# Two expert layers of a fused network: spread shared by two engines, operands loaded ahead, the second layer dense over all tokens

## The chip, the cores and the metric

One program runs on one core of one Trainium2 chip. The metric is the device time of one execution in microseconds (us). The core has five engines that each work through their own queue in order: PE (TensorE, matrix products; PEld is its weight load), DVE (VectorE), ACT (ScalarE), POOL (GpSimd) and SP (SyncE, which here issues nearly all transfers). Transfers go through 16 DMA engines.

## The reference

The network is two blocks. The first has two layers over 256 context tokens and 256 latent tokens of width 1024; each layer is a token mixer and then an expert layer (`peer_ffn`). The second block (four layers of attention or recurrence, each with a gated feed-forward part) is not touched here. An expert layer computes, per token, 8 heads x 16 chosen experts out of 16384:

```python
qr = (h @ wq).reshape(bsz, t, 8, 2, 128)
scores = jnp.einsum('bthpd,hpkd->bthpk', qr, subkeys)
s1, i1 = lax.top_k(scores[..., 0, :], 16)
s2, i2 = lax.top_k(scores[..., 1, :], 16)
cand = (s1[..., :, None] + s2[..., None, :]).reshape(bsz, t, 8, 256)
cidx = (i1[..., :, None] * 128 + i2[..., None, :]).reshape(bsz, t, 8, 256)
top, pos = lax.top_k(cand, 16)
eidx = jnp.take_along_axis(cidx, pos, axis=-1)
gate = jax.nn.softmax(top, axis=-1)
act = jax.nn.gelu(jnp.einsum('ted,td->te', u[ek], hk), approximate=False)
out = jnp.einsum('te,ted->td', gk * act, v[ek])
```

The first layer's expert part handles 512 tokens (context and latent), the second layer's the 256 latent ones only.

## The kernel before, in words

Every expert layer is computed in two ways at once (`peer`, line 883). The first F tokens are **gathered**: `fetched` (line 858) reads, per token, the 128 chosen rows of u and v with one indirect transfer on POOL's queue (tile `uv`, line 873) and does two passes over 1024 columns on DVE (lines 874 and 869). The other ND = N - F tokens are **dense**: all 16384 experts are computed for them, as 128 rows j of 128 experts, and a gate matrix that is zero where an expert was not chosen removes the rest. `FETCHED` sets F: 128 of 512 tokens in the first expert layer, 64 of 256 in the second.

Work of one expert layer, in the order of the code:

- `route` (line 719): 16 chunks of queries and scores, top-16 searches on DVE (`top16`), the choice of experts per tile of 128 tokens (`choose`), the gate values (`gates`), and `spread` (line 813). Spread builds the dense gate matrix four tokens at a time: a one-hot tile `oa` of 512 columns and four scaled one-hot tiles `ob` of 128 columns, all on DVE (lines 819 and 824), four small products on PE (line 825), and two copies out on ACT (line 828), written to DRAM tile `g` every 32 tokens.
- `ahead` (line 958) runs the **first product** of one row j beside the routing: a load `wraw` of u, and the products with all ND tokens on PE. In the first expert layer u is split into a coarse part `whi` (ACT) and a rest `wlo` (DVE), and 24 products of 384 columns follow, in threes of whi, whi, wlo (line 949). In the second layer ND is 192, the sum `xw` is used, and 8 full-precision products run without a split (line 944). The result goes to DRAM tile `u`.
- After the routing a **dense loop** goes over pairs of rows j: `u_phase` (line 983) loads gates (`gt`) and first products (`ad`) four rows at a time, applies Gelu on ACT, multiplies on DVE and splits the result into `wt`; rows that were not done ahead are computed here. `v_phase` (line 1008) loads a row of v (`wraw`, line 1013), splits it and runs the **second product**. With ND a multiple of 128 it is token-stationary: `wt` holds the weights, v streams with 512 columns (line 1026, 18 products a row in the first layer). Otherwise v holds the weights and `wt` streams with 192 columns (line 1019, 24 products a row).

What orders the work: the loop over `route` keeps two sums of estimated times, `tp` for PE and `td` for DVE, and calls `ahead` while `tp` is behind `td`; `EVERY` does the same for the gathered tokens, and what is left of those goes evenly over the dense loop. A scheduler then places the instructions of each engine; buffers rotate, so a load waits until the buffer's last reader is done.

Of the kernel before, what the change touches and what calls it, by code (L numbers as in the profile page):

```python
# [41 lines left out]
CU = (.0108, .0137)  # L42
# [4 lines left out]
FETCHED = (128, 64)  # L47
# [4 lines left out]
WORKP = (dict(nbig=2048, bufs=4, ga=3, w=(4, 3, 2), mm=2, sm=6, sp=4, uv=4, H=1, acc=1),  # L52
         dict(nbig=2048, bufs=2, ga=3, w=(6, 2, 2), mm=4, sm=4, sp=6, uv=5, H=1, acc=1, xw=1))
ROUTE = dict(bufs=3, rt=1, VI=1, t=3, r=13, alt=1, oa=2, ob=4)
DENSE = dict(bufs=1, gt=2, ad=2, wt=2, o=2)
# [28 lines left out]
class Kern:  # L84
# [634 lines left out]
    def route(self, l, xh, xl, cs, G, F, fetch):  # L719
# [93 lines left out]
        def spread(t):  # L813
            for t0 in range(*own(t), GT):
                st = [self.b8().rearrange("p (j t) -> p j t", t=GT) for _ in range(2)]
                for t4 in range(t0, t0 + GT, 4):
                    pg = self.ps()
                    a = self.t(512, tag="oa").rearrange("p (t n) -> p t n", t=4)
                    nc.vector.tensor_tensor(a, self.iotaf[:, None, :].to_broadcast([P, 4, P]),
                                            i1T[:, t4:t4 + 4, None].to_broadcast([P, 4, P]), op=OP.is_equal)  # L820
                    for i in range(4):
                        t_ = slice(t4 + i, t4 + i + 1)
                        b_ = self.t(P, tag="ob")
                        nc.vector.tensor_scalar(b_, self.iotaf, i2T[:, t_], gT[:, t_], op0=OP.is_equal, op1=OP.mult)
                        nc.tensor.matmul(pg[:, i * P:(i + 1) * P], a[:, i], b_, start=True, stop=True)
# [57 lines left out]
    def peer(self, l, extra=()):  # L883
# [8 lines left out]
        xh, xl = self.big(KD, N, F32R), self.big(KD, N, F32R)  # L892
# [35 lines left out]
        self.part(routing, **ROUTE)  # L928
# [9 lines left out]
        def u_act(j, func):  # L938
            ps = self.ps("MM")[:, :ND]
            if whole:  # L940
                raw = self.w.tile([P, 1024], F32, name="wraw", bufs=self.wb[0])
                nc.sync.dma_start(raw, A["uT"][l, j])
                for k in range(KD):
                    nc.tensor.matmul(ps, raw[:, k * P:(k + 1) * P], xw[:, k], start=k == 0, stop=k == KD - 1)  # L944
            else:
                hi, lo = self.load_w(A["uT"][l, j])
            for k in range(0 if whole else KD):
                for q, (w_, x_) in enumerate(((hi, xh), (hi, xl), (lo, xh))):
                    nc.tensor.matmul(ps, w_[:, k * P:(k + 1) * P], x_[k, dc],  # L949
                                     start=(k == 0 and q == 0), stop=(k == KD - 1 and q == 2))  # L950
            a = self.t(max(ND, D // 2), tag="ga")[:, :ND]
            self.actv(a, ps, func)
            return a


        early, tp, td = 0, 0.0, HEAD[l]

        def ahead():
            nc.sync.dma_start(U[:, early], u_act(early, AF.Copy))
        done = 0  # L960
        for pe, dve in self.route(l, xh, xl, cs, G, F, fetch):
# [3 lines left out]
            while tp < td and early < P:  # L965
                ahead()
                early, tp, td = early + 1, tp + ND * CU[l], td + (0.0 if whole else 1.1)
# [6 lines left out]
        self.part(dense, **DENSE)  # L974
        left = F - done
        J = 2

        nd = ND // P if ND % P == 0 else 0
        res = [[self.ps() for _ in range(2)] for _ in range(nd)] if nd else [self.ps() for _ in range(4)]
        half = lambda c: res[c // 2][:, c % 2 * 256:c % 2 * 256 + ND]  # L980
        held = {}

        def u_phase(j0):
            if j0 % 4 == 0:
                gt = self.t(4 * ND, tag="gt")
                held["g"] = gt.rearrange("p (b j t) -> p j b t", j=4, t=GT)
                nc.sync.dma_start(gt.rearrange("p (b j) -> p b j", b=nb),
                                  G[:, :nb, j0:j0 + 4].rearrange("p b j t -> p b (j t)"))
                if j0 < early:
# [1002 lines left out]
```

## Time and profile before

| what | value |
|---|---|
| runs of the kernel | 4761.98, 4771.15, 4781.52 us (median 4771.15) |
| the profiled execution | 4776.65 us; its span from first to last instruction 4774.9 us |
| busy over the span | PE 4352.2 us (91%), DVE 3402.8 (71%), ACT 2104.5 (44%), POOL 288.9 (6%) |
| mean granted TensorE clock | 0.953 of 2.4 GHz |
| moved | 948.85 MB, mean 199 GB/s |

The span has these stages, read from the first and last instruction of the lines above: first mixer to 385 us; first expert layer, routing and first product, 385 to 1240, its dense loop 1240 to 1836; second mixer to 2086; second expert layer, routing 2086 to 2436, its dense loop 2436 to 3108; the second block from there to the end. A share of the whole span says little here; each stage has to be read on its own.

### The profile page before, as it was taken

Reading aid. Unit: us, or ns where it says so; the run is one execution under the profiler, and the core shown is the slowest. Engines: PE = TensorE matmul, PEld = TensorE weight load, DVE = VectorE, ACT = ScalarE, POOL = GpSimd, SP = SyncE. Lnnn points to the kernel's source line nnn. Section 1 sums busy time; section 2 is a strip of 40 time slices with the busy share of each in tenths; the row PEclk is TensorE's granted clock in tenths of the full one; section 3 lists DMA queues with packets and bytes.
Section 4 is the critical chain, followed back from the end, with each engine's and each line's share of the span. In section 5 each row is a group of like instructions: output and inputs, shape, how many; then the busy total and the mean of one; then the engine's idle time right before and its main releaser. Section 6 shows DMA issues by size and latency. Waiting matters only on the chain. (4 is left out here: it accounts for less than half of the span.)

```text
span 4774.9 us, 72861 instructions
## 1 busy us (share of the span) xinstructions
PE 4352.2 (91%) x27964; PEld 3992.4 (84%) x27964; DVE 3402.8 (71%) x6651; ACT 2104.5 (44%) x4022; POOL 288.9 (6%) x200
## 2 busy tenths in 40 slices
PE   6999798998988999998967799989999999999999
PEld 5887798888876787887856699978998998899799
DVE  9987998899778757978863344477567567566765
ACT  4443344344433445541323233377445454445853
POOL 0000022222011100001220000000000000000000
PEclk8999899999999999999977799999999998999999
DMA  5413388888999874547994468533553553055255
GB/s 191 133 58 104 136 291 323 295 309 329 327 305 337 281 223 130 169 160 282 377 376 146 148 204 266 193 99 103 175 152 108 175 159 100 19 172 165 90 168 172
DMA packets 313101, 948.85 MB, mean 199 GB/s; under 512 B 28832, under 2 KB 130080, under 8 KB 282928
## 3 DMA queue, kind: packets, MB, share of 16 engines
q1 hardware_dynamic: 285104, 742.86, 47.4%
q0 software_dynamic: 27648, 201.34, 11.2%
q8 instruction: 219, 3.59, 0.3%
q14 instruction: 130, 1.06, 0.1%
HBM read 872.70 MB, written 71.04 MB: 198 GB/s over the span
## 5 line engine op out<-in xcount | busy, mean ns | idle before, releaser
L208 ACT ACTIVATE whi<-wraw 128x1024 fp32r<-128x1024 f32 (+1 forms) x924 | 964.3, 1047 | 1337.0 <-PE MM L293 524.3
L293 PE MATMUL MM<-xhl,whi 128*128 128x272 f32 (+1 forms) x4736 | 934.6, 293 | 6.7 <-ACT whi L208 6.1
L275 DVE TENSOR_TENSOR wlo<-wraw,whi 128x1024 fp32r<-128x1024 f32 (+2 forms) x668 | 799.3, 1198 | 161.2 <-PE MM L293 53.1
L293 PE MATMUL MM<-b,whi 128*128 128x272 f32 (+2 forms) x3712 | 855.3, 323 | 59.8 <-ACT b L208 50.0
L293 PEld LDWEIGHTS MM<-xhl,whi 128*128 128x128 f32 x4736 | 751.2, 190 | 27.4 <-issue 10.0
L293 PEld LDWEIGHTS MM<-b,whi 128*128 128x128 f32 x3712 | 623.0, 192 | 115.8 <-ACT b L208 56.5
L293 PE MATMUL MM<-xhl,wlo 128*128 128x272 f32 (+1 forms) x2368 | 689.2, 291 | 2.8 <-DVE wlo L275 2.7
L293 PE MATMUL MM<-b,wlo 128*128 128x272 f32 (+2 forms) x1856 | 597.2, 323 | 5.3 <-DVE wlo L275 4.7
L949 PE MATMUL MM<-b,whi 128*128 128x384 f32 x2048 | 545.4, 347 | 14.2 <-ACT ga L208 13.9
L280 DVE TENSOR_TENSOR wlo<-wraw,whi 128x1024 fp32r<-128x1024 f32 x256 | 311.3, 1222 | 277.4 <-ACT whi L208 206.4
L1019 PE MATMUL SM<-wt,whi 128*128 128x192 f32 x2048 | 399.0, 300 | 103.2 <-ACT whi L208 76.1
L293 PEld LDWEIGHTS MM<-xhl,wlo 128*128 128x128 f32 x2368 | 448.7, 190 | 10.2 <-DVE wlo L275 4.6
L873 POOL DMA_INDIRECT uv<-uv,sp x192 | 287.9, 1499 | 2676.1 <-DVE acc L869 952.0
L1019 PEld LDWEIGHTS SM<-wt,whi 128*128 128x128 f32 x2048 | 352.6, 215 | 106.9 <-ACT whi L208 79.3
L949 PE MATMUL MM<-b,wlo 128*128 128x384 f32 x1024 | 356.0, 349 | 59.0 <-DVE wlo L275 59.0
L949 PEld LDWEIGHTS MM<-b,whi 128*128 128x128 f32 x2048 | 380.2, 195 | 18.6 <-ACT ga L208 17.9
L1026 PE MATMUL SM<-whi,wt 128*128 128x512 f32 x1536 | 380.7, 397 | 13.7 <-ACT wt L208 8.0
L293 PEld LDWEIGHTS MM<-b,wlo 128*128 128x128 f32 x1856 | 355.7, 192 | 31.2 <-DVE wlo L275 10.0
L944 PE MATMUL MM<-xw,wraw 128*128 128x192 f32 x2048 | 359.1, 332 | 10.5 <-ACT ga L208 9.9
L1026 PEld LDWEIGHTS SM<-whi,wt 128*128 128x128 f32 x1536 | 293.7, 192 | 82.1 <-ACT wt L208 10.7
L944 PEld LDWEIGHTS MM<-xw,wraw 128*128 128x128 f32 x2048 | 339.7, 194 | 12.5 <-ACT ga L208 11.6
L1019 PE MATMUL SM<-wt,wlo 128*128 128x192 f32 x1024 | 305.0, 298 | 15.2 <-DVE wlo L280 15.2
(488 smaller groups left out, 6096.8 us busy)
## 6 DMA issues: line engine op xcount, KB each, us to landing
wraw<-uT SPq DMA_DIRECT2D x256, 512.0 KB
wraw<-uv SPq DMA_DIRECT2D x256, 512.0 KB
wraw<-w_gate_up SPq DMA_DIRECT2D x176, 512.0 KB
g<-b SPq DMA_DIRECT2D x36, 1024.0 KB
wraw<-w_in SPq DMA_DIRECT2D x64, 512.0 KB
wraw<-fox_w_in SPq DMA_DIRECT2D x64, 512.0 KB
wraw<-w_down SPq DMA_DIRECT2D x64, 512.0 KB
wmod<-wmodT SPq DMA_DIRECT2D x56, 512.0 KB
```

The lines of the kernel that those rows point to most:

```text
L208: r = nc.scalar.activation(out, in_, func, **kw)
L275: nc.vector.tensor_sub(lo[:, :n], raw[:, :n], hi[:, :n].bitcast(F32))
L280: self.nc.vector.tensor_sub(lo, src, hi.bitcast(F32))
L293: nc.tensor.matmul(ps, w_, x_[k, slice(a, b)], start=(i == 0 and q == 0), stop=(i == kc - 1 and q == 2))
L873: nc.gpsimd.indirect_dma_start(z, None, self.A[f"uv{l}"], bass.IndirectOffsetOnAxis(ap=ids[:, js], axis=0))
L944: nc.tensor.matmul(ps, raw[:, k * P:(k + 1) * P], xw[:, k], start=k == 0, stop=k == KD - 1)
L949: nc.tensor.matmul(ps, w_[:, k * P:(k + 1) * P], x_[k, dc], start=(k == 0 and q == 0), stop=(k == KD - 1 and q == 2))
L1019: nc.tensor.matmul(half(c), w_[:, c * P:(c + 1) * P], x_[:, jj], start=j == 0 and q == 0 and c % 2 == 0, stop=j == P - 1 and q == 2, skip_ ...
L1026: nc.tensor.matmul(res[c][h], w_[:, jj, c * P:(c + 1) * P], v[:, h * 512:(h + 1) * 512], start=(j == 0 and q == 0 and i == 0), stop=(j == ...
```

## The change

- `FETCHED` becomes (128, 0): the second expert layer gathers no tokens, and all its 256 tokens are dense. Since 256 is a multiple of 128 and above 192, its first product takes the split form (24 products of 256 columns) and its second product the token-stationary one (12 products of 512 columns a row).
- All 128 rows of the first product are done before the dense loop, in both layers; the last ones after the routing has ended. Gelu is applied as the product leaves PSUM. The products with `whi` all come first, then those with `wlo`.
- Spread: both one-hot tiles are built on DVE with 512 columns, and the scaling by the gate moves to ACT (four instructions of 128 columns for four tokens). The `oa` ring has 3 buffers in the first layer and 4 in the second.
- The dense loop loads v rows 4 (first layer) or 5 (second) rows ahead into buffers of its own (`vr`), gates 8 rows at a time and one group ahead, first products 4 rows at a time and two groups ahead.
- The normalised inputs `xh`, `xl` now lie in the memory that is freed at the end of the routing part.

```diff
-CU = (.0108, .0137)
+CU = (.0108, .0113)
-FETCHED = (128, 64)
+FETCHED = (128, 0)
-ROUTE = dict(bufs=3, rt=1, VI=1, t=3, r=13, alt=1, oa=2, ob=4)
-DENSE = dict(bufs=1, gt=2, ad=2, wt=2, o=2)
+ROUTE = (dict(bufs=7, rt=1, VI=1, t=3, r=13, alt=1, oa=3, ob=2), dict(bufs=5, rt=1, VI=1, t=4, r=16, alt=2, oa=4, ob=2, xw=1))
+DENSE = (dict(bufs=0, gt=2, ad=3, wt=2, vr=5, o=2), dict(bufs=0, gt=2, ad=3, wt=2, vr=6, o=2))
+LAST = 4
...
-                    a = self.t(512, tag="oa").rearrange("p (t n) -> p t n", t=4)
-                    nc.vector.tensor_tensor(a, self.iotaf[:, None, :].to_broadcast([P, 4, P]),
-                                            i1T[:, t4:t4 + 4, None].to_broadcast([P, 4, P]), op=OP.is_equal)
+                    ohs = []
+                    for z in (i1T, i2T):
+                        o = self.t(512, tag="oa")
+                        nc.vector.tensor_tensor(o.rearrange("p (t n) -> p t n", t=4),
+                                                self.iotaf[:, None, :].to_broadcast([P, 4, P]),
+                                                z[:, t4:t4 + 4, None].to_broadcast([P, 4, P]), op=OP.is_equal)
+                        ohs.append(o)
+                    b_ = self.t(512, tag="ob")
                     for i in range(4):
-                        t_ = slice(t4 + i, t4 + i + 1)
-                        b_ = self.t(P, tag="ob")
-                        nc.vector.tensor_scalar(b_, self.iotaf, i2T[:, t_], gT[:, t_], op0=OP.is_equal, op1=OP.mult)
-                        nc.tensor.matmul(pg[:, i * P:(i + 1) * P], a[:, i], b_, start=True, stop=True)
+                        ts = slice(i * P, (i + 1) * P)
+                        self.actv(b_[:, ts], ohs[1][:, ts], AF.Copy, scale=gT[:, t4 + i:t4 + i + 1])
+                        nc.tensor.matmul(pg[:, ts], ohs[0][:, ts], b_[:, ts], start=True, stop=True)
...
+                terms = [(hi[:, k * P:(k + 1) * P], z[k, dc]) for k in range(KD) for z in (xh, xl)]
+                terms += [(lo[:, k * P:(k + 1) * P], xh[k, dc]) for k in range(KD)]
+            for i, (w_, x_) in enumerate(terms):
+                nc.tensor.matmul(ps, w_, x_, start=i == 0, stop=i == len(terms) - 1)
             a = self.t(max(ND, D // 2), tag="ga")[:, :ND]
-            self.actv(a, ps, func)
-            return a
+            self.actv(a, ps, AF.Gelu)
+            nc.sync.dma_start(U[:, j], a)
...
-            while tp < td and early < P:
+            while tp < td and early < P - LAST:
                 ahead()
...
-        late = min(P, -(-early // 4) * 4 + 4)
-        while early < late:
+        while early < P:
             ahead()
-            early += 1
+            done += fetch_for(ND * CU[l], 10.0)
...
+        J, JU, JG = 2, 4, 8
+        def load_g(n):
+            if n < P // JG:
+                gt = self.t(JG * ND, tag="gt")
+                nc.sync.dma_start(gt.rearrange("p (b j) -> p b j", b=nb),
+                                  G[:, :nb, n * JG:(n + 1) * JG].rearrange("p b j t -> p b (j t)"))
+        def load_u(n):
+            if n < P // JU:
+                ads[n] = self.t(JU * ND, tag="ad").rearrange("p (j t) -> p j t", j=JU)
+                nc.sync.dma_start(ads[n], U[:, n * JU:(n + 1) * JU])
+        def load_v(j):
+            if j < P:
+                raws[j] = self.t(D, tag="vr")
+                nc.sync.dma_start(raws[j], A[f"uv{l}"].rearrange("(p j) d -> p j d", j=P)[:, j, D:])
+        def gated(j0):
+            if j0 % JG == 0:
+                load_g(j0 // JG + 1)
+            if j0 % JU == 0:
+                load_u(j0 // JU + 2)
+            wt = self.t(J * 2 * ND, F32R, "wt").rearrange("p (j s t) -> p j s t", j=J, s=2)
+            for jj in range(J):
+                nc.vector.tensor_mul(b3(a[:, jj]), b3(a[:, jj]), gts[j0 // JG][:, j0 % JG + jj])
+            self.split(a, wt[:, :, 0], wt[:, :, 1])
+            return wt
```

Three places in the engines' queues show what this does.

VectorE in the second expert layer, at the end of the spread (`oa`, `ob` are the one-hot tiles, `acc`, `ga` the two passes of a gathered token, `wlo` the split of a loaded row, `ad` first products times gates). Before:

```order
L819 TENSOR_TENSOR oa<-iotaf,rt 128x512
L824 TENSOR_SCALAR ob<-iotaf,rt 128x128 x4
L874 SCALAR_TENSOR_TENSOR ga,sp<-uv,H 128x1024
L869 SCALAR_TENSOR_TENSOR acc<-uv,sp,acc 128x1024
L819 TENSOR_TENSOR oa<-iotaf,rt 128x512
L824 TENSOR_SCALAR ob<-iotaf,rt 128x128 x4
L280 TENSOR_TENSOR wlo<-wraw,whi 128x1024 x2
```

And now:

```order
L823 TENSOR_TENSOR oa<-iotaf,rt 128x512 x20
L277 TENSOR_TENSOR wlo<-wraw,whi 128x1024
L823 TENSOR_TENSOR oa<-iotaf,rt 128x512 x2
L277 TENSOR_TENSOR wlo<-wraw,whi 128x1024
L823 TENSOR_TENSOR oa<-iotaf,rt 128x512 x8
L277 TENSOR_TENSOR wlo<-wraw,whi 128x1024 x81
L1015 TENSOR_TENSOR ad<-ad,gt 128x256 x4
```

The gathered tokens are gone, few splits of u stand among the spread, and 81 of the 128 rows of the first product come after it, ahead of the dense loop.

SyncE at the start of the second layer's dense loop (`gt` gates, `ad` first products, `wraw` or `vr` rows of v, `u` and `g` the DRAM tiles). Before:

```order
L831 DMA g_66<-b_20186 128x2048
L959 DMA u_68<-ga 128x192 x2
L1013 DMA wraw<-uv 128x1024
L987 DMA gt<-g_66 128x6x128
L991 DMA ad<-u_68 128x768
L987 DMA gt<-g_66 128x6x128
L991 DMA ad<-u_68 128x768
L1013 DMA wraw<-uv 128x1024
```

And now:

```order
L964 DMA u_68<-ga 128x256 x7
L993 DMA gt<-g_66 128x8x256
L964 DMA u_68<-ga 128x256
L999 DMA ad<-u_68 128x1024 x2
L1004 DMA vr<-uv 128x1024 x5
L993 DMA gt<-g_66 128x8x256
L999 DMA ad<-u_68 128x1024
```

Rows of v were already loaded before the loop began; now the first gates, first products and five rows of v are issued together at its start, and none of them earlier, since their buffers lie in the memory of the routing part.

TensorE at the end of the first product in the first expert layer (`b` are the tiles of the normalised input). Before:

```order
L949 MATMUL MM<-b_2890,whi 128x384
L949 MATMUL MM<-b_2892,whi 128x384
L949 MATMUL MM<-b_2890,wlo 128x384
L1026 MATMUL SM<-whi,wt 128x512 x12
L1026 MATMUL SM<-wlo,wt 128x512 x6
```

And now:

```order
L961 MATMUL MM<-b_2899,whi 128x384
L961 MATMUL MM<-b_2901,whi 128x384
L961 MATMUL MM<-b_2898,wlo 128x384 x4
L961 MATMUL MM<-b_2899,wlo 128x384 x4
L1031 MATMUL SM<-whi,wt 128x512 x12
L1031 MATMUL SM<-wlo,wt 128x512 x6
```

The eight products that need the rest `wlo` moved from every third place to the end of the row.

## Rows read from the trace of the kernel before

**Rows 1.** Windows: stretch, length, then busy us of each engine, clock, DMA, GB/s.

```profile
385.00:1240.00 855.00, 769.26 (x4370) 730.12 (x4371) 751.38 (x1770) 332.39 (x712) 150.37 (x92) 0.96 0.73 261
1240.00:1640.00 400.00, 354.67 (x1454) 279.13 (x1453) 321.39 (x431) 162.62 (x245) 58.33 (x36) 0.96 0.91 318
1640.00:1836.00 196.00, 195.58 (x874) 162.21 (x873) 97.09 (x117) 84.62 (x93) 0.00 (x0) 1.00 0.64 204
2086.00:2436.00 350.00, 305.89 (x1964) 295.29 (x1964) 296.28 (x807) 99.58 (x306) 51.31 (x43) 0.93 0.81 301
2436.00:2500.00 64.00, 27.72 (x140) 25.98 (x139) 42.49 (x61) 15.94 (x44) 21.30 (x14) 0.63 0.99 371
2500.00:2786.00 286.00, 203.84 (x1386) 197.64 (x1385) 100.73 (x147) 84.08 (x117) 0.00 (x0) 0.77 0.48 154
2786.00:3108.00 322.00, 322.00 (x2472) 322.00 (x2472) 150.16 (x222) 115.27 (x212) 6.56 (x7) 1.00 0.71 229
```

**Rows 2.** Waits from 2500 to 2786 us: who for whom, us, times, longest.

```profile
ACT ad L208 <- DMA ad<-u: 109.5, 15, 13.2
ACT whi L208 <- PE SM L1019: 95.2, 28, 4.8
PE SM L1019 <- ACT whi L208: 74.4, 15, 6.6
```

**Rows 3.** Groups of instructions on VectorE, the same stretch.

```profile
L280 DVE TENSOR_TENSOR wlo<-wraw,whi 128x1024 fp32r<-128x1024 f32 x58 | 69.7, 1223 | 90.2 <-ACT whi L208 90.2
```

**Rows 4.** Timeline of PE, four places: start, us, instruction.

```profile
1225.32 0.33 PE L949 MATMUL MM<-b,wlo 128*128 128x384 f32 x1
1227.92 0.33 PE L949 MATMUL MM<-b,wlo 128*128 128x384 f32 x1
...
1824.86 2.88 PE L1026 MATMUL SM<-whi,wt 128*128 128x512 f32 x12
1828.94 2.88 PE L1026 MATMUL SM<-whi,wt 128*128 128x512 f32 x12
...
2100.41 0.28 PE L293 MATMUL MM<-b,wlo 128*128 128x256 f32 x1
2100.77 0.28 PE L293 MATMUL MM<-b,wlo 128*128 128x256 f32 x1
...
2907.02 0.27 PE L1019 MATMUL SM<-wt,wlo 128*128 128x192 f32 x1
2910.37 0.27 PE L1019 MATMUL SM<-wt,wlo 128*128 128x192 f32 x1
```

**Rows 5.** Groups of instructions, second expert layer's routing, 2086 to 2436 us.

```profile
L824 DVE TENSOR_SCALAR ob<-iotaf,rt 128x128 f32<-128x128 f32 x192 | 53.9, 354 | 4.2 <-PE SM L825 4.1
L874 DVE SCALAR_TENSOR_TENSOR ga<-uv,H 128x1024 bf16<-128x1024 f32 x39 | 47.5, 1218 | 33.5 <-DMA u<-ga 24.7 <-issue 6.4 <-ACT b L208 1.3
L869 DVE SCALAR_TENSOR_TENSOR acc<-uv,sp,acc 128x1024 f32<-128x1024 f32 x37 | 47.3, 1279 | 7.7 <-ACT sp L208 7.7
L819 DVE TENSOR_TENSOR oa<-iotaf,rt 128x512 f32<-128x512 f32 x48 | 32.8, 683 | 0.0
L275 DVE TENSOR_TENSOR wlo<-wraw,whi 128x1024 fp32r<-128x1024 f32 x14 | 16.9, 1208 | 5.4 <-ACT whi L208 5.4
L208 ACT ACTIVATE b<-SM 128x256 f32<-128x256 f32 x95 | 31.2, 385 | 54.6 <-PE SM L825 28.3 <-DMA g<-b 26.3
```

**Rows 6.** Groups of instructions, first expert layer's routing, 385 to 1240 us.

```profile
L949 PE MATMUL MM<-b,wlo 128*128 128x384 f32 x1024 | 356.0, 349 | 59.0 <-DVE wlo L275 59.0
L824 DVE TENSOR_SCALAR ob<-iotaf,rt 128x128 f32<-128x128 f32 x384 | 110.5, 351 | 7.4 <-PE SM L825 4.4 <-PE MM L949 3.0
L208 ACT ACTIVATE whi<-wraw 128x1024 fp32r<-128x1024 f32 x143 | 151.4, 1059 | 355.3 <-PE MM L949 252.2 <-PE MM L293 47.1 <-DMA wraw<-uT 44.4
L208 ACT ACTIVATE rt<-SM 128x128 f32<-128x128 f32 x9 | 1.8, 280 | 0.0
```

**Rows 7.** Windows again, the last 100 us of the second layer's routing.

```profile
2336.00:2436.00 100.00, 88.08 (x569) 83.65 (x568) 86.66 (x189) 30.28 (x111) 20.60 (x18) 0.98 1.00 391
```

More of the change, by code (lines that the diff above doesn't have):

```diff
@@ L926, in fetch_for @@
             return n
-        self.part(routing, **ROUTE)
+        self.part(routing, **ROUTE[l])
+        xh, xl = self.big(KD, N, F32R), self.big(KD, N, F32R)
         parts = [(0, T, M(1, 4), M(1, 3))] if N == 512 else []
@@ L936, in peer, with ahead @@
             nc.vector.tensor_add(xw, xh.all3(KD)[:, :, dc].bitcast(F32), xl.all3(KD)[:, :, dc].bitcast(F32))
-        def u_act(j, func):
+        early, tp, td = 0, 0.0, HEAD[l]
+        def ahead():
+            nonlocal early
+            j = early
+            early += 1
             ps = self.ps("MM")[:, :ND]
@@ L1010, in v_phase, with products @@
+        def products(j0, wt):
             for jj in range(J):
                 j = j0 + jj
-                raw = self.w.tile([P, 1024], F32, name="wraw", bufs=self.wb[0])
-                nc.sync.dma_start(raw, A[f"uv{l}"].rearrange("(p j) d -> p j d", j=P)[:, j, D:])
+                load_v(j + VR)
                 vh, vl = (self.w.tile([P, 1024], F32R, name=n, bufs=b) for n, b in zip(("whi", "wlo"), self.wb[1:]))
-                self.split(raw, vh, vl)
-                if not nd:
-                    for c in range(KD):
-                        for q, (w_, x_) in enumerate(((vh, wh), (vh, wl), (vl, wh))):
-                            nc.tensor.matmul(half(c), w_[:, c * P:(c + 1) * P], x_[:, jj],
-                                             start=j == 0 and q == 0 and c % 2 == 0, stop=j == P - 1 and q == 2,
-                                             skip_group_check=True)
@@ new lines, in products @@
+                first, end = j == 0, j == P - 1
+                if nd:
+                    for q, ss, v in ((0, (0, 1), vh), (1, (0,), vl)):
+                        for c in range(nd):
+                            for h in range(2):
+                                for s_ in ss:
+                                    nc.tensor.matmul(res[c][h], wt[:, jj, s_, c * P:(c + 1) * P],
+                                                     v[:, h * 512:(h + 1) * 512], start=first and q == 0 and s_ == 0,
+                                                     stop=end and q == 1)
+                else:
+                    both = wt[:, jj].rearrange("p s t -> p (s t)")
+                    for c in range(KD):
+                        nc.tensor.matmul(res[c][:, :2 * ND], vh[:, c * P:(c + 1) * P], both, start=first, stop=end,
+                                         skip_group_check=True)
+                    for c in range(KD):
+                        nc.tensor.matmul(res[c][:, :ND], vl[:, c * P:(c + 1) * P], wt[:, jj, 0], start=False, stop=end,
+                                         skip_group_check=True)
@@ L1038, in peer @@
+        products(*prev)
         for _ in chain(extra, *steps):
```

95 lines of the change are left out of this document (34 added, 61 removed).

## The prediction

> **What bounds the kernel now.** I cut the span into stages with the windows view first, since the shares of the whole page mix them. The first expert layer's routing has PE busy 769 of 855 us and DVE 751, so two in-order engines hand work to each other and each is idle about a tenth [rows 1]. The first 400 us of its dense loop sit against the transfers (DMA engines busy 0.91), while its last 196 us are all PE [rows 1]. In the second layer's routing DVE (296 of 350 us) is again close to the length. The surprise is its dense loop: from 2500 to 2786 us nothing is full. PE is busy 204 of 286 us at a granted clock of 0.77 of 2.4 GHz (part of it at the lower level of 1.2), DVE 101, the DMA engines 0.48, and yet from 2786 on the same loop runs with PE full and the clock at 1.00 [rows 1].
>
> The waits view says why. ACT waits 109.5 us for the load of first products, and behind that wait in its queue stand the splits of v that PE needs; ACT also waits 95.2 us for PE to free a split buffer, and PE 74.4 us for ACT [rows 2]. So this stretch is bound by a chain of latencies. 58 splits of v in 286 us [rows 3] are one row j per 4.93 us, against 24 products of 192 columns at 0.112 us (3.35 us for 30, [rows 4]), or 2.68 us, of PE work.
>
> **The change, part by part.** Pitches on PE, all from [rows 4]: 0.173 us for 384 columns (2.60 us for 15), 0.227 for 512 (4.08 for 18), 0.120 for 256 (0.36 for 3).
>
> *Second layer, routing with first product.* DVE's 296 us lose the gathered tokens (47.5 + 47.3) and the old spread (53.9 + 32.8) [rows 5]. They gain the new spread, 256 tokens / 4 = 64 groups x 2 x 0.683 = 87 us, and the splits of the 47 rows of u that the order places before the end of the spread, 47 x 1.21 = 57 us. That makes 259 us. Inside the spread ACT now does more than DVE. Per group it has two copies out (31.2 us for 95, so 0.33 each, [rows 5]) and four scaled copies of 128 columns, which no row shows; the nearest is `rt<-SM` of 128x128, 1.8 us for 9 back to back, 0.20 each, and 0.28 alone [rows 6]. I take 0.25, since they will often wait for one another; the ends are worth 64 x 4 x 0.05 = 13 us down and 8 up. Per group 1.66 us, 106 us in all, and 10 rows of u at 1.4 us (split 1.06, [rows 6], copy out 0.35) beside it: 120 us, against DVE's 87 + 11 x 1.21 = 100. So 20 us more: 279 us. Before, the stage took 350 for 296 us of DVE work, 1.18 times [rows 1]; by that 329 us.
>
> The Trainium skill, "ScalarE: Activation LUTs", section "What ACT_TABLE_LOAD costs", gives an instruction with a pointer operand 280 ns + 0.833 ns per column, less 93 ns of overlap, which is 0.294 us at 128 columns; by it, an estimate, this term would be 13 us longer. No run here shows it.
>
> The other 81 rows of u come after the routing, with PE alone as the limit: 24 x 0.120 = 2.88 us, 233 us. ACT (1.4 us a row) and DVE (1.2) lie beside it. Then a hole: gates, first products and v are issued only when the last first product has left its inputs' memory. 1.6 MB for the first pair at the 391 GB/s of [rows 7] are 4 us, and then a multiply, two splits on ACT and DVE and the split of v follow, some 8 us: 12. Bounds: 4 if only the load shows; 36, the idle PE time at this place before (64 - 28, [rows 1]).
>
> *Second layer, dense loop.* 128 rows x 12 x 0.227 = 349 us on PE. Per row DVE has 1.22 for v [rows 3], half of that for the split of `wt` (1024 columns for two rows) and at most 0.4 for the gates (256 columns against 0.683 for 512, [rows 5]), 2.2 us in all; ACT 1.06 and half of that, 1.6; both below 2.72. The transfers are 0.79 MB a row, 289 GB/s, against 391 reached [rows 7]. What made the stall is gone by construction if loads run ahead: the gates and first products are asked for at least four rows (11 us) early, where the longest wait for them was 13.2 us with no such lead [rows 2]. I take 355 us, and 5 for the end. Bounds: 349, and 128 x 3.0 = 384 should 10% of the old stall stay.
>
> Sum for the layer: 329 + 233 + 12 + 355 + 5 = 934 us instead of 1022 (2086 to 3108): **-88**. Bounds -150 (no factor 1.18, hole 4) and 0.
>
> *First layer, routing.* DVE's spread falls from 110.5 us for `ob` [rows 6] and 96 x 0.683 = 66 for `oa` [rows 5] to 192 x 0.683 = 131 us: -45 us of 751. PE idles 59 us for `wlo` [rows 6]; with the 16 products of `whi` first it has 16 x 0.173 = 2.8 us of work while DVE makes it. ACT takes on 96 x 4 x 0.25 = 96 us, into 523 us of idle time [rows 1]. New is a wait: each group needs two `oa` tiles of a ring of three, so DVE's second tile waits until PE has used the tile of the group before, and PE may be inside a row of u (24 x 0.173 = 4.2 us). I take **-35**; bounds -75 (PE's 86 us of idle time nearly gone) and +20.
>
> *First layer, dense loop.* Same bytes, so the transfers allow 400 x 0.91 = 364 us; PE's floor there is 1454 products [rows 1] / 18 = 81 rows x 4.08 = 330. Gates in twice longer pieces may cost the DMA engines less, but no row shows the price by piece. A hole as above, 13 us, opens at the start. The last 196 us stay. 364 + 13 - 400 = -23; I take **-20**; bounds -65 and +13. Gelu moves to another place on ACT, which waits anyway; four more table loads and the second layer's end cost a few us, inside the terms.
>
> Total -35 - 20 - 88 = -143. The profiled execution took 4776.65 us (span 4774.9), 5.5 above the median of the runs shown. 4776.65 - 143 = 4634, and set against the median **4628 us**.
>
> **The rivals.** *All engines fed.* Hand-overs between DVE, ACT and PE vanish with deeper rings: first layer -60 and -50, second layer 1.05 x 279 = 293 instead of 329 and a hole of 5: 4776 - 60 - 50 - 131 = 4535, or **4530** by the median. For it: PE full after 2786 us. Against it: DVE and PE both near 90% in the first layer stay coupled.
>
> *The ring of three decides.* If each of the 96 groups costs DVE one more us than now in the first layer (half of the mean 2.1 us that PE still needs when inside a row), 96 us come on top: **4724**. For it: old waits of DVE on PE were only 7.4 us [rows 6], with rings that let a group overlap. Against it: DVE has other work queued between the two tiles.
>
> *The loop stays paced by latency: slower.* In the new dense loop of the second layer the same in-order queues remain: ACT's splits of v stand behind the split of `wt`, that behind the load of first products. If a row keeps the old 4.93 us, the loop takes 631 us instead of 355: 4628 + 276 = **4904**. It decides from 2.72 + 143/128 = 3.8 us a row on. For it: the old loop starved with the DMA engines half idle. Against it: the deeper loads, and 391 GB/s with many transfers in flight. [...]
>
> *Nothing gained:* the second layer's extra PE work (first and second product of 64 more tokens) and ACT's spread eat the stall that is removed: about 4771.
>
> **How the numbers follow.** Forecast 0.64, all fed 0.13, ring 0.12, nothing 0.05, paced loop 0.06. The forecast's own bounds are some 4580 to 4700; taking in the ring and the near half of the fed case gives 4545 to 4730. Half a per cent (24 us) is about what a measurement of this kernel tells from no change: faster 0.64 + 0.13 + 0.12 = 0.89, the same 0.05, slower 0.06.
>
> **What would show it.** In the new profile: the second layer's dense loop near 2.75 us a row with PE full and the clock at 1.00; a stretch of some 230 us of first products before it with PE full; PE idle 10 to 15 us between them; ACT busiest in the second layer's spread, about 1.7 us per group; fewer waits of PE on `wlo` in the first layer. Wrong would be: rows in the dense loop above 3.8 us, DVE waiting on PE at the second `oa` tile for more than 100 us, or a first layer that does not get shorter.

## The result and the profile after

The changed kernel takes 4621.08 us (median of 4 runs, 4615.89 to 4624.64), the kernel before 4766.56 (4 runs on the same chip): a ratio of 0.9689, 95% interval [0.9663, 0.9714]. The profiled execution of after took 4615.89 us, 160.8 less than that of before, at a mean granted clock of 0.974.

Windows of after, cut at the same events as [rows 1] (last first product, first and last second product, last product of the spread); columns as there:

```profile
385.00:1206.00 821.00, 756.91 (x4369) 724.55 (x4369) 712.47 (x1479) 448.35 (x1095) 141.34 (x93) 0.97 0.76 272
1206.00:1224.00 18.00, 0.42 (x1) 0.42 (x2) 16.04 (x28) 3.52 (x7) 1.68 (x1) 0.61 0.98 352
1224.00:1600.00 376.00, 348.64 (x1492) 283.83 (x1492) 307.01 (x413) 135.71 (x200) 57.82 (x34) 0.96 0.90 337
1600.00:1784.00 184.00, 184.00 (x813) 152.35 (x812) 89.02 (x101) 64.71 (x67) 0.00 (x0) 1.00 0.55 183
2037.00:2110.00 73.00, 71.12 (x562) 67.59 (x560) 69.10 (x299) 34.83 (x59) 0.00 (x0) 1.00 0.48 144
2110.00:2210.00 100.00, 97.88 (x792) 95.49 (x791) 99.87 (x185) 56.62 (x96) 0.00 (x0) 1.00 0.70 214
2210.00:2331.00 121.00, 103.13 (x715) 93.26 (x713) 85.52 (x126) 119.32 (x382) 0.00 (x0) 0.99 0.47 175
2331.00:2565.00 234.00, 233.53 (x1944) 233.32 (x1944) 99.26 (x81) 108.48 (x163) 0.00 (x0) 1.00 0.72 224
2565.00:2576.00 11.00, 0.00 (x0) 0.00 (x0) 3.51 (x9) 3.95 (x5) 0.00 (x0) 0.67 0.90 317
2576.00:2941.00 365.00, 355.69 (x1537) 289.18 (x1537) 230.51 (x312) 167.76 (x192) 0.00 (x0) 0.99 0.81 270
```

The reader is to see three things. The first layer ends at 1784 instead of 1833 us: 34 us from its routing and 15 from its loop, in which PE now stands still for 18 us at the start. The second layer's routing goes from full DVE (to 2210) to full ACT (119 of 121 us) to full PE (from 2331). And the stretch with nothing full, 2500 to 2786 in [rows 1], is gone: the loop's 128 rows take 365 us, 2.85 each, with PE busy 356.

Waits in that loop, against [rows 2]:

```profile
ACT whi L210 <- PE SM L1031: 181.4, 121, 2.9
DVE ad L1015 <- DMA ad<-u: 59.1, 21, 4.0
PE SM L1031 <- ACT whi L210: 11.2, 1, 11.2
```

ACT now waits for PE; PE's one wait for ACT is the hole at the start. The load of first products is still waited for, by DVE instead of ACT.

The last 121 us of the second layer's spread, groups of instructions (against [rows 5]), and one burst of scaled copies from the timeline of ACT:

```profile
L210 ACT ACTIVATE ob<-oa,rt 128x128 f32<-128x128 f32 x240 | 77.3, 400 | 0.0
L823 DVE TENSOR_TENSOR oa<-iotaf,rt 128x512 f32<-128x512 f32 x117 | 76.1, 689 | 32.0 <-ACT ob L210 29.1 <-ACT rt L210 2.0 <-PE SM L831 0.8
L210 ACT ACTIVATE b<-SM 128x256 f32<-128x256 f32 x119 | 39.5, 383 | 1.5 <-PE SM L831 0.9
...
2252.08 1.86 ACT L210 ACTIVATE ob<-oa,rt 128x128 f32<-128x128 f32 x6
```

A scaled copy occupies ACT for 77.3 / 240 = 0.32 us. That is a mean: copies that follow one another start 0.29 us apart (six in 1.86 us, the last with its full 0.39), and the next instruction of another kind starts some 0.4 us after the last of them. DVE's wait at the `oa` ring is for ACT (29.1 us), hardly for PE (0.8).

PE's waits in the first layer's routing, 385 to 1206 us (against [rows 6]):

```profile
PE SM L831 <- ACT ob L210: 28.5, 21, 7.1
PE MM L961 <- DVE wlo L277: 15.8, 8, 10.6
PE MM L961 <- ACT ga L210: 15.4, 5, 5.8
```

The 59 us for `wlo` fell to 16; the spread's products now wait 28.5 us for ACT.

### The profile page after: what moved, and what is told of

The parts are those of the page before. It is cut to its first block, busy times and chain, and to the rows that moved or that the text cites. A ratio compares the mean times of both kernels' runs of the same rounds, so it can differ in the third digit from the quotient of the medians.

```text
span 4614.1 us, 72517 instructions
## 1 busy us (share of the span) xinstructions
PE 4335.8 (94%) x27588; PEld 3930.0 (85%) x27588; DVE 3361.9 (73%) x6146; ACT 2361.9 (51%) x4572; POOL 201.9 (4%) x136
## 5 line engine op out<-in xcount | busy, mean ns | idle before, releaser
L210 ACT ACTIVATE whi<-wraw 128x1024 fp32r<-128x1024 f32 (+2 forms) x796 | 831.2, 1045 | 927.0 <-PE MM L295 547.3
L295 PEld LDWEIGHTS MM<-b,whi 128*128 128x128 f32 x3712 | 620.7, 191 | 113.9 <-ACT b L210 57.5
L961 PE MATMUL MM<-b,whi 128*128 128x384 f32 (+1 forms) x4096 | 677.7, 315 | 19.9 <-ACT ga L210 17.0
L1031 PE MATMUL SM<-whi,wt 128*128 128x512 f32 x2560 | 628.0, 392 | 29.0 <-ACT whi L210 29.0
L961 PEld LDWEIGHTS MM<-b,whi 128*128 128x128 f32 x4096 | 624.4, 193 | 24.0 <-ACT ga L210 19.4
L1031 PEld LDWEIGHTS SM<-whi,wt 128*128 128x128 f32 x2560 | 484.8, 189 | 131.7 <-ACT whi L210 29.5
L210 ACT ACTIVATE whi<-vr 128x1024 fp32r<-128x1024 f32 x256 | 271.2, 1059 | 395.0 <-PE SM L1031 363.7
L282 DVE TENSOR_TENSOR wlo<-vr,whi 128x1024 fp32r<-128x1024 f32 x256 | 311.9, 1220 | 113.1 <-ACT whi L210 96.0
L295 PEld LDWEIGHTS MM<-b,wlo 128*128 128x128 f32 x1856 | 354.5, 191 | 31.8 <-DVE wlo L277 10.6
L1031 PE MATMUL SM<-wlo,wt 128*128 128x512 f32 x1280 | 340.1, 396 | 36.6 <-DVE wlo L282 36.6
L961 PE MATMUL MM<-b,wlo 128*128 128x384 f32 (+1 forms) x2048 | 352.5, 312 | 18.1 <-DVE wlo L277 18.1
L961 PEld LDWEIGHTS MM<-b,wlo 128*128 128x128 f32 x2048 | 313.5, 190 | 23.4 <-DVE wlo L277 23.1
L1031 PEld LDWEIGHTS SM<-wlo,wt 128*128 128x128 f32 x1280 | 241.0, 190 | 96.9 <-DVE wlo L282 47.8
```

What stands on the lines that cost most here:

```text
L210: r = nc.scalar.activation(out, in_, func, **kw)
L282: self.nc.vector.tensor_sub(lo, src, hi.bitcast(F32))
L295: nc.tensor.matmul(ps, w_, x_[k, slice(a, b)], start=(i == 0 and q == 0), stop=(i == kc - 1 and q == 2))
L961: nc.tensor.matmul(ps, w_, x_, start=i == 0, stop=i == len(terms) - 1)
L1031: nc.tensor.matmul(res[c][h], wt[:, jj, s_, c * P:(c + 1) * P], v[:, h * 512:(h + 1) * 512], start=first and q == 0 and s_ == 0, stop=end ...
```

## The experiments

The theory behind the prediction: early loads end the stall of the second dense loop, and DVE's lighter spread shortens the first layer. Rivals: the dense, token-stationary form does it by itself; and the first layer's gain is that of the order of `whi` and `wlo`. From each profiled execution the table gives, in us, the start of the first layer's last first product, of its last second product, and the length from there to the second layer's last second product (the second mixer, about 253 us, included).

| kernel | us, median | ratio to before [95%] | last first product | first layer ends | from there to end of second |
|---|---|---|---|---|---|
| before | 4766.56 | | 1239.8 | 1832.8 | 1274.7 |
| after | 4621.08 | 0.9689 [0.9663, 0.9714] | 1205.4 | 1784.0 | 1156.6 |
| before, second layer dense | 4654.01 | 0.9752 [0.9736, 0.9769] | 1237.4 | 1829.2 | 1149.8 |
| after, 64 gathered | 4658.19 | 0.9761 [0.9745, 0.9777] | 1210.0 | 1793.1 | 1189.9 |
| after, all loads late | 4760.52 | 0.9972 [0.9963, 0.9982] | 1209.1 | 1832.6 | 1265.1 |
| after, old spread | 4615.29 | 0.9676 [0.9660, 0.9692] | 1209.8 | 1794.2 | 1144.8 |
| after, old order | 4660.73 | 0.9777 [0.9759, 0.9794] | 1230.2 | 1811.4 | 1169.3 |
| after, more rows in the spread | 4585.43 | 0.9621 [0.9602, 0.9639] | 1204.3 | 1791.6 | 1119.9 |
| after, second layer's loads in own memory | 4610.43 | 0.9669 [0.9651, 0.9686] | 1211.3 | 1797.8 | 1154.1 |
| both of these | 4572.10 | 0.9591 [0.9574, 0.9609] | 1208.3 | 1795.6 | 1113.8 |
| after, gates and first products late | 4652.31 | 0.9759 [0.9732, 0.9785] | 1206.8 | 1798.3 | 1174.0 |
| after, v late | 4763.03 | 0.9994 [0.9981, 1.0006] | 1209.3 | 1827.2 | 1264.2 |
| before, new order | 4781.52 | 1.0028 [1.0013, 1.0043] | 1249.8 | 1836.9 | 1271.7 |
| before, new order, two `whi` | 4748.83 | 0.9944 [0.9927, 0.9960] | 1210.3 | 1802.2 | 1278.4 |

Each ratio is to runs of before in the same session (medians 4765 to 4772 us), so a difference of two medians from different sessions can be off by some 7 us. The last three columns are of one execution each.

### The dense form alone, in the kernel before

```diff
-FETCHED = (128, 64)
+FETCHED = (128, 0)
-CU = (.0108, .0137)
+CU = (.0108, .0113)
```

> The kernel before, with one thing changed: the second expert layer gathers no tokens, all 256 are dense (first product in the split form, second product token-stationary with 512 columns); the old dense loop with its old loads, and the old spread. Theory A (the stall of the old loop is a chain of latencies, and only loads that run ahead remove it): the rows done ahead still pass the loop at 4 to 5 us each, so the second layer falls from 1022 us by 10 to 60 only. Rival B (the token-stationary product and the absence of gathered tokens are what matters): the second layer falls to about 910 us as in the changed kernel, some 110 us.

Measured: 4654.01 us, 118 less than before: rival B is right. The second layer (with the mixer) takes 1149.8 us, 125 less, and so is no longer than in the changed kernel (1156.6), with none of the new leads, only the old six load buffers that u and v share. (With no gathered tokens, the step that adds them at the end is left out.) Windows of its dense loop, to 2600 and to 2968 us:

```profile
2376.00:2600.00 224.00, 210.85 (x1073) 178.78 (x1072) 130.88 (x171) 112.65 (x153) 0.00 (x0) 0.98 0.80 256
2600.00:2968.00 368.00, 368.00 (x2367) 336.71 (x2366) 207.89 (x263) 176.50 (x261) 0.00 (x0) 1.00 0.66 207
```

After 2600 each row has its first product in the loop, 5.6 us of PE work, under which every load hides. But the earlier rows, most of them without it, are fed too (PE 211 of 224 us, where before it had 204 of 286): the first 50 rows take 151 us, 3.0 each, where the first 70 of before took 340, 4.9 each. Only 52 rows are done ahead instead of 72, and the rest have their first product in the loop. So the kernel with the dense form and nothing else of the change has the stall no more.

Why its early rows are fed is not shown by a run of its own, but SyncE's queue has a likely cause. `gt` are the gates and `ad` the first products of one group of four rows, `wraw` the loads of v. Before:

```profile
2606.70 0.53 SPq L987 DMA_DIRECT2D gt<-g  x1
2608.12 10.37 SPq L1013 DMA_DIRECT2D wraw<-uv  x4
2618.63 1.03 SPq L991 DMA_DIRECT2D ad<-u  x1
```

and with the dense form alone:

```profile
2480.77 0.53 SPq L987 DMA_DIRECT2D gt<-g  x1
2482.03 1.47 SPq L1013 DMA_DIRECT2D wraw<-uv  x2
2483.77 0.33 SPq L991 DMA_DIRECT2D ad<-u  x1
2485.30 3.04 SPq L1013 DMA_DIRECT2D wraw<-uv  x2
```

In the code, gates and first products of a group are asked for one right behind the other; the scheduler put four loads of v between them before, and two at most here. SyncE waits at a load of v until a split has freed a buffer (139 us in the stretch of [rows 2]), so that before the first products were asked for 11 to 13 us after the gates in all groups from 2500 us on, and with the dense form 1 to 7 us. ACT then waited 6.5 to 7.7 us for nearly every group before, and 0.5 to 4.9 us here. That this order of issues, and not the form of the product, is what feeds the early rows was not tried by itself.

Against the gain, 64 more tokens cost PE little: the second product takes 12 x 0.227 = 2.72 us a row instead of 24 x 0.112 = 2.69 ([rows 4]), the first 2.88 instead of 2.54 (two rows in 5.08 us of the timeline of before), 47 us for 128 rows.

### The rest of the change alone: 64 tokens still gathered

```diff
-FETCHED = (128, 0)
+FETCHED = (128, 64)
-CU = (.0108, .0113)
+CU = (.0108, .0137)
```

> The changed kernel, with 64 of the 256 tokens of the second layer gathered as before (first product in 8 full-precision products of 192 columns, second product with v as weights: 8 products of 384 and 8 of 192 columns a row). Theory A: the deep loads alone free the dense loop; a row costs 8 x 0.173 + 8 x 0.112 = 2.3 us there, and the second layer takes 820 to 900 us, no longer than the 904 of the changed kernel. Rival B: without the dense form the gain of the second layer is gone; it takes 980 us or more, and the whole is 75 us or more slower than the changed kernel.

Measured: 4658.19 us, and the second part 1189.9 us, 85 less than before and 33 more than after. That lies between the two texts: without the mixer the layer takes some 937 us, where theory A wanted 900 at most and rival B 980 at least. Each half of the change wins most of the second layer's gain; they replace one another (125 and 85 apart, 118 together). This half is more than early loads, though. It has the new spread and all first products ahead, and its second product is a third form of 16 products a row (8 of 384 columns, 8 of 192), which at [rows 4]'s pitches is 2.28 us a row, less than the 2.69 of before. Its loop takes 416 us all the same (3.25 a row) at a granted clock of 0.89; PE waits there 78 us for DVE's `wlo`.

The second layer's routing in the kernel with the dense form alone, and in this one:

```profile
2082.00:2376.00 294.00, 267.69 (x2078) 255.24 (x2077) 280.70 (x808) 132.70 (x279) 0.00 (x0) 0.98 0.57 182
2049.00:2381.00 332.00, 294.18 (x1895) 284.35 (x1895) 271.27 (x657) 150.45 (x488) 57.32 (x43) 0.96 0.83 306
```

The first takes 1.05 times DVE's busy time (third figure), the second 1.22 times, where the kernel before took 1.18 times.

### Which load has to be early

```diff
-DENSE = (dict(..., ad=3, ..., vr=5, ...), dict(..., ad=3, ..., vr=6, ...))
+DENSE = (dict(..., ad=2, ..., vr=2, ...), dict(..., ad=2, ..., vr=2, ...))
-                load_g(j0 // JG + 1)
+                load_g(j0 // JG)
-                load_u(j0 // JU + 2)
+                load_u(j0 // JU)
...
-        load_g(0)
-        load_u(0)
-        load_u(1)
```

> The changed kernel with shallow loads in both dense loops: one row of v ahead (2 buffers), gates and first products asked for only when their group begins (2 buffers each). Theory A: the second layer's loop goes from 365 us (2.85 a row) to 3.8 us a row or more, 490 to 630 us, and the first layer's loop from 561 to 590 or more: 120 to 300 us slower than the changed kernel, granted clock well below 1.00 in the second layer's loop. Rival B: depth hardly matters once the product is token-stationary: within 30 us of the changed kernel.

Measured: 4760.52 us; 139 us of the 145 are lost, as theory A said, with a loop of 471 us just short of its range and a clock of 0.96 there, hardly below 1.00. This kernel mixes two leads, so each was taken away by itself: gates and first products late (all edits but those of `DENSE`), and v late (only the two `vr=2`).

> The changed kernel with v still loaded 4 or 5 rows ahead, but gates and first products asked for only when their rows come up. Theory A (the prediction's: the old stall was the wait for gates and first products, 109.5 us in the trace of before; their lead is what removes it): at least 80 of the 139 us that the kernel with all loads shallow lost come back as a loss, 4700 us or more, with long waits for the load of first products in the second dense loop. Theory B (in that kernel the wait was for v, 255 us of it in the second loop, and v's lead is what counts): a loss of at most 40 us, 4621 to 4660.

> The changed kernel with gates and first products still asked for a group or two ahead, but v only one row ahead (two buffers instead of 5 or 6). Theory A: a loss of at most 40 us, 4621 to 4660. Theory B: nearly the whole loss of the kernel with all loads shallow, 4720 to 4770, with ACT waiting for v some 200 us in the second dense loop. If the two leads only cover for each other, both this kernel and the one with late gates stay within 60 us of the changed kernel.

Measured: 4652.31 us with gates and first products late, a loss of 31; 4763.03 with v late, a loss of 142, all of it. Theory B of both texts is right. Waits in the second dense loop with late gates and first products:

```profile
ACT whi L210 <- PE SM L1031: 164.4, 115, 3.5
DVE ad L1015 <- DMA ad<-u: 101.4, 30, 9.6
PE SM L1031 <- ACT wt L210: 20.8, 1, 20.8
```

and with late v:

```profile
ACT whi L210 <- DMA vr<-uv: 261.2, 120, 5.2
DVE wlo L282 <- ACT whi L210: 224.8, 115, 4.9
PE SM L1031 <- ACT whi L210: 86.3, 77, 11.2
```

In the first, DVE waits 101 us for first products, as ACT did before, but ACT with the splits of v stays ahead of PE, and PE waits for ACT once, at the start (20.8 us instead of 11.2), besides 16.5 us for `wlo` (9.2 in after). In the second, ACT waits for 120 of 128 rows of v. This is a lead that the change must keep, and not one that it brought to the second layer: the old kernel had six load buffers there, and in the stalled stretch, whose rows have no first product in the loop, nothing waited for v (in the view that [rows 2] is from, no wait is for v). In the first layer, with four load buffers, ACT did wait 89.3 us for v in the loop of before, and waits 13.5 us in after.

### The spread's move to ACT

```diff
-                    ohs = []
...
+                    a = self.t(512, tag="oa").rearrange("p (t n) -> p t n", t=4)
...
+                        nc.vector.tensor_scalar(b_, self.iotaf, i2T[:, t_], gT[:, t_], op0=OP.is_equal, op1=OP.mult)
```

> The changed kernel with the spread of before in both layers (both one-hot tiles on DVE, none of it on ACT, rings of 2 and 4). Theory A: the first layer's routing (821 us) gets back the 35 us that the shorter DVE work gave, the second layer's spread (121 us, paced by ACT) stays about as long, 64 x 1.83 = 117 us of DVE: 20 to 45 us slower in all. Rival C (the first layer's gain came from the order of whi and wlo, DVE time is hidden there): within 10 us of the changed kernel.

Measured: 4615.29 us, the same as after (intervals overlap): rival C is right. The last first product of the first layer starts 4 us later than in after (1209.8 to 1205.4), with DVE again as busy as before the change (third figure, 752 us; 751 in [rows 1]):

```profile
385.00:1210.00 825.00, 760.12 (x4369) 720.82 (x4369) 751.91 (x1769) 346.53 (x711) 146.75 (x94) 0.97 0.74 269
```

So DVE's relief there is worth nothing that can be measured: what DVE wins, PE then waits for at ACT. With the old spread PE waits 33.1 us for `wlo`, 26.6 for the copy out and 0.4 for the spread; in after it is 15.8, 15.4 and 28.5, so 60.1 and 59.7 us in all. The second part is 12 us shorter with the old spread (1144.8 us).

### The order of the first products

```diff
-                terms = [(hi[:, k * P:(k + 1) * P], z[k, dc]) for k in range(KD) for z in (xh, xl)]
-                terms += [(lo[:, k * P:(k + 1) * P], xh[k, dc]) for k in range(KD)]
+                terms = [(w_[:, k * P:(k + 1) * P], z[k, dc]) for k in range(KD)
+                         for w_, z in ((hi, xh), (hi, xl), (lo, xh))]
```

> The changed kernel with the old order within a row of the first product (whi, whi, wlo in threes instead of all whi first). Theory A: PE again waits some 40 us for wlo in the first layer's routing, but DVE is nearly full there, so only a part is lost: 5 to 20 us slower. Rival C (that order is the first layer's gain): 30 us or more slower.

Measured: 4660.73 us, 40 more than after, which is rival C's number; the last first product of the first layer comes 25 us later, PE waits 33 us for `wlo` there, and the second part is 13 us longer. The order matters. Then the opposite: only the order put into the kernel before, and, since that gained nothing, the order with one buffer of `whi` less in the first layer. That ring's cut, `w=(4, 3, 2)` to `w=(4, 2, 2)`, is in the change too, and the prediction had not looked at it.

```diff
-            for k in range(0 if whole else KD):
-                for q, (w_, x_) in enumerate(((hi, xh), (hi, xl), (lo, xh))):
+            turns = [(k, q) for k in range(KD) for q in (0, 1)] + [(k, 2) for k in range(KD)]
+            for k, q in [] if whole else turns:
+                w_, x_ = ((hi, xh), (hi, xl), (lo, xh))[q]
...
```

> The kernel before, with one edit: of a row's 24 first products the 16 with the coarse part come first, then the 8 with the rest. Theory A (the order is what shortened the first layer's routing, not the spread's move to ACT): the routing part, 385 to 1240 us before, ends 20 to 40 us earlier, PE's wait for the rest falls from 59 us to under 25, and the time is 4720 to 4750. Theory B (DVE with its old spread stays the slower engine there, so that PE then waits for other work of DVE): within 10 us of before.

> The kernel before with the new order of the first products and, in the first layer, the ring of coarse parts cut from three buffers to two, as the changed kernel has it. Theory A (with three buffers ACT runs ahead with the next rows' splits, waits there for loads and for DVE, and the copy that frees PE's PSUM stands behind; order and shorter ring together shorten the first layer's routing): PE's wait for the copy out falls from 47 us to under 20, the last first product ends 25 to 45 us earlier than with the order alone (1250 us), and the time is 4725 to 4755. Theory B (the shorter ring is not the missing piece, the changed kernel's other pieces are): 4765 us or more.

Measured: the order alone gives 4781.52 us, 0.3% slower than before; theory B's number was nearer, but not its reason. PE's wait for `wlo` did fall, from 59.0 to 26.0 us; another took its place, that for the copy out (`ga`), 47.0 us where before it was 13.9. With the shorter ring it is 4748.83 us: theory A of the second text is right, and the last first product comes 39.5 us earlier than with the order alone (1249.8 to 1210.3). Waits of PE and ACT in the first layer's routing, order alone:

```profile
PE MM L950 <- ACT ga L208: 47.0, 18, 5.9
PE MM L950 <- DVE wlo L275: 26.0, 26, 7.9
...
ACT whi L208 <- DMA wraw<-uT: 120.6, 33, 10.0
```

and with two buffers of `whi`:

```profile
PE MM L950 <- DVE wlo L275: 28.3, 28, 7.9
PE MM L950 <- ACT ga L208: 14.6, 9, 5.1
...
ACT whi L208 <- DMA wraw<-uT: 14.8, 4, 6.7
```

With three, ACT takes up splits of rows whose load is not there yet (120.6 us), and the copy that frees PE's PSUM stands behind them in its queue: in 18 of the 47 us that PE waits for it, ACT is itself waiting for such a load, and with two buffers in none. With two, a split waits for PE (86.9 us instead of 57.3) or for DVE's `wlo` (97.4 instead of 68.6), and the copy comes through. The rest of the 47 us is not traced. Neither piece does it alone: the order without the shorter ring ends the first products 10 us later than before, the shorter ring with the old order (in the changed kernel, the run above) 10 us earlier, both together 29.5.

### Making more of it

In after, ACT sets the pace of the second layer's spread (119 of 121 us) while 81 rows of u wait for the time behind it. The estimated costs of a group of the spread, which the loop adds to `tp` and `td`, decide how many rows go in between:

```diff
-                    yield 1.3, 1.6
+                    yield (1.3, 1.6) if F else (.9, 2.4)
```

> The changed kernel with other estimates for one step of the second layer's spread (0.9 us for PE and 2.4 for the busier engine instead of 1.3 and 1.6), so that more rows of the first product stand among the spread: about 50 instead of 10, and some 40 instead of 81 after it. Theory A: the spread is paced by ACT (119 of 121 us busy) while PE has time left, ACT has 1.45 us of work for a row against 2.9 of PE; the spread gets longer but less so than the rest gets shorter: 15 to 35 us faster than the changed kernel. Rival D (every row's split and copy out on ACT comes on top of a full engine, and hand-overs eat the rest): no change within 8 us.

Measured: 4585.43 us, 36 less than after, just past theory A's upper end. Its windows, from the start of the second layer's spread stretch to its loop's start:

```profile
2110.00:2417.00 307.00, 303.00 (x2533) 300.19 (x2532) 245.13 (x378) 233.08 (x563) 0.00 (x0) 1.00 0.70 230
2417.00:2532.00 115.00, 115.00 (x961) 115.00 (x959) 47.20 (x39) 52.13 (x79) 0.00 (x0) 1.00 0.68 217
2532.00:2543.00 11.00, 0.55 (x4) 0.35 (x3) 3.85 (x10) 3.98 (x5) 0.00 (x0) 0.66 0.88 312
```

PE is full from 2110 to 2532 but for 4 us; 39 rows are left behind the spread instead of 81. Next, the hole of 11 us: gates, first products and v of the second layer got memory of their own (that of `acc`, which no token uses there any more, and of a smaller `ga`), so that their loads need not wait for the end of the routing part.

```diff
-         dict(nbig=2048, ..., H=1, acc=1))
+         dict(nbig=2048, ..., H=1, acc=1, gt=2, ad=3, vr=5))
...
-... dict(bufs=0, gt=2, ad=3, wt=2, vr=6, o=2))
+... dict(bufs=0, wt=2, o=2))
...
```

> The changed kernel with the second layer's gates, first products and rows of v in memory of their own, so that their loads can start before the last first product is done (5 buffers of v instead of 6, and some unused tiles left out to make room). Theory A: the 11 us hole before the second layer's loop closes to 2 to 4 us and the clock stays up: 7 to 12 us faster. Rival E (the hole is the chain of multiply, splits and hand-overs, not the loads): at most 3 us faster.

> The two edits before together (other estimates for the spread, loads of the second layer in memory of their own). Theory A: both gains add, 25 to 45 us faster than the changed kernel. Rivals D and E together: within 10 us.

Measured: 4610.43 us alone, which the intervals do not separate from after, so that theory A and rival E stay open for the time. The hole did close, from 11.2 to 1.0 us, so it was the loads; the loop behind it took 370 us in this execution, 365 in that of after and 367 to 369 in three others with the old hole. Both together: 4572.10 us, 49 less than after and a little past theory A, ratio 0.9591 [0.9574, 0.9609] against 0.9689 [0.9663, 0.9714]. It is the fastest version seen, and beats both kernels.

## Why the prediction was right, and where its steps were not

The sum was -143 us. By the medians the change is 145 (4621 for 4628), by the profiled executions, to which the terms belong, 161. The second layer's routing won 35 us more than forecast, its loop and the first layer's two terms 16 less; the layer's end, taken at 5 us, took 6 with all that follows. That the medians meet the forecast this closely is in part luck: the profiled execution of before lies 10 us above its median, that of after 5 below. The time held, but two of the reasons given for it fell.

- **Second layer's routing, 329 us: 294.** DVE's work was as counted (69 + 100 + 86 = 255 us, forecast 259), and in the last stretch ACT was the limit: the spread took 129 us from its first product to its last, forecast 120. The step that failed is the factor 1.18 from the old stage, put on top of the 20 us that had been added for ACT. Of the 39.5 us that DVE idles now, 35.5 lie in ACT's stretch; in the 173 us before it DVE is busy 169. [Rows 5] could have told: 41 of the 54 us that DVE idled there stood in front of the two passes of gathered tokens (33.5 and 7.7), and those passes are what was removed. The same stage of two other kernels bears it out (the two lines under the run with 64 tokens gathered): its length over DVE's work is 1.05 without gathered tokens and 1.22 with them. The scaled copy had been taken at 0.25 us and cost 0.32 in the mean; back to back it is 0.29. The Trainium skill ("ScalarE: Activation LUTs", section "What ACT_TABLE_LOAD costs") has figures from which 0.294 us is estimated for such an instruction at 128 columns, and the trace agrees with it back to back. By that estimate the term would have been 11 us longer, where the prediction wrote 13.
- **81 rows of u, 233 us: 234. Hole, 12: 11.** Right.
- **Second dense loop, 355 us: 365.** The size held within its bounds, PE waiting 9 us for `wlo`; the cause, "gates and first products are asked for at least four rows early", did not. Taking their lead away costs 31 us in the whole kernel, at both layers; cutting v to two buffers costs 142, but v had its lead in the stalled loop already. The dense form alone fed the loop with none of the new leads. ACT's 109.5 us in [rows 2] was the right place to look, but removing a wait from the queue that holds the splits also did part of it: in after Gelu runs before the store, so that DVE waits for first products, and that wait (101 us when late) starves nobody. That this move is what makes their lateness cheap is argued from the waits and was not tried by itself.
- **First layer's routing, -35 us: -34.** The number held, its reason ("-45 us of 751" of DVE's work) did not: with the old spread the first products end 4 us later and the whole takes the same time. It is the order together with the shorter ring of `whi`: -29.5 us in the kernel before. The prediction did name PE's idle time for `wlo` and the 2.8 us of cover; that half stands.
- **First layer's loop, -20 us: -15.** Hole 17.9 instead of 13. With late gates and first products the loop and its hole take 591.5 us (before 593.0, after 578.6), so what it won seems to hang on their lead; the other kernels with that lead took 581 to 587, so it is worth 4 to 13 us. One old loop took 587.2 (before with the new order), so part of this is the spread of single executions.
- **The rivals.** The ring of three: in the first layer's routing DVE waits 0.2 us at it for PE, where more than 100 would have shown it. Nothing gained would have been 4771. The paced loop: 2.85 us a row instead of 3.8 or more, but it came within reach once v was late: 472 us for 128 rows, 3.7 each, which the prediction did not see as the lever. All engines fed: after is 91 us from it, the best version 42.

Open: whether the dense form feeds the early rows of the loop by its form or by the order of issues that came with it. In the kernel with that form alone ACT waited 35 us for first products up to 2600 us, where before it waited 109.5, and they were asked for sooner after the gates, as shown above; no run here separates the two.

## What to carry over

When two parts of a change each remove the same stall, test each alone: here the dense form by itself and all the rest without it gave 125 and 85 us in the second layer, and together no more than the first. Read the queue that issues the loads as well as the engine that waits for one: a load can be late because it stands behind others that wait for buffers. Before a stage's idle share is carried over as a factor, look at which instructions it stands in front of; it leaves with them. A deeper ring is not always better on an engine that works through its queue in order: with a third buffer and the new order of products, ACT took up splits whose data had not come and held up the copy that PE waited for.

## What the runs showed of the hardware

A hole in PE's work can cost more than its length. Timeline of PE in the best version, the first layer's loop after a hole of 18.72 us, and a later row:

```profile
1227.33 5.49 PE L1031 MATMUL SM<-whi,wt 128*128 128x512 f32 x12 [18.72 <-ACT whi L210]
...
1234.33 2.88 PE L1031 MATMUL SM<-whi,wt 128*128 128x512 f32 x12
```

and windows of the hole, of that first row, and of the 7 us behind it:

```profile
1209.00:1227.00 18.00, 0.00 (x0) 0.00 (x0) 13.46 (x23) 3.10 (x6) 0.77 (x1) 0.61 0.97 348
1227.00:1233.00 6.00, 5.67 (x13) 4.51 (x14) 4.41 (x7) 1.33 (x2) 0.00 (x0) 0.50 0.99 329
1233.00:1240.00 7.00, 7.00 (x32) 5.78 (x31) 5.59 (x7) 3.25 (x5) 2.62 (x2) 0.98 1.03 414
```

The first 12 products took 2.6 us longer than the same 12 one row later. After 18 us in which PE did nothing the row ran at a granted clock of 0.50, the lower level of 1.2 GHz, and by the next row it was back at the upper one. In the second layer of the same kernel, where the hole is 1.0 us, the clock stayed at 1.00 and the first 8 products took 2.28 us against 1.98 later:

```profile
2538.86 2.28 PE L1031 MATMUL SM<-whi,wt 128*128 128x512 f32 x8 [0.99 <-ACT wt L210]
...
2544.63 1.98 PE L1031 MATMUL SM<-whi,wt 128*128 128x512 f32 x8
```

That 24 products of 192 columns take 2.69 us and 12 of 512 take 2.72 (0.112 and 0.227 each) was in [rows 4] from the start: a third more tokens for the same PE time. The prediction used both numbers and never set them side by side. They are why the second product of 64 more tokens costs PE next to nothing.
